# Gates behind the values' products, an output projection by single blocks, and a second norm summed inside the second FFN chunk

## The chip, the cores and the metric

The kernel runs on one core of one Trainium2 chip. The metric is the time of one execution on the device in microseconds. The median of three runs of the kernel before is 382.78 us (382.38 to 382.90).

## What is computed

A decoder layer for 256 tokens of 1,024 channels, all in float32. With one layer, one sequence and a block of 256 tokens, both attentions are plain causal softmax attentions over the 256 tokens:

```python
h = rms_norm(x, attn_norm_g)
qa, ka, va, qb, kb, vb, f_logit, g_logit = split(h @ w_in)      # 6 x 512, 8, 2 x 1024 columns
o_a = attention(rope(norm(qa)), rope(norm(ka)), va)              # 8 heads of 64, "MoBA"
o_b = attention(norm(qb), norm(kb), vb, bias=cumsum(log_sigmoid(f_logit + b_forget)))   # 8 heads, "FoX"
gates = sigmoid(g_logit + b_gate)                                # two gates for each channel
merged = gates[0] * (o_a @ w_branch_moba) + gates[1] * (o_b @ w_branch_fox)
x = x + merged @ w_out
h2 = rms_norm(x, ffn_norm_g)
u, g = split(h2 @ w_ffn_up)                                      # 2 x 2816 columns
x = x + (silu(causal_conv3(g)) * u) @ w_ffn_down
```

## The kernel before

Every large product is done in the type float32r with operands split in two: `hi` is the operand copied to float32r, `lo` is what the copy lost, and three products (hi·hi, hi·lo, lo·hi) are added in PSUM. Activations lie with channels on the partitions and the 256 tokens along the row, so that weights are the 128x128 stationary operand and a product moves 256 columns. In the first projections (q, k, v) it is the other way round, with 512 columns.

Weights come in chunks of 1 MB (128 x 2048), by one DMA each on SyncE's queue, into one of three buffers `raw`. A chunk is split in two halves, each by ScalarE (`whi`, line 122) and VectorE (`wlo`, line 123). Six buffers of each hold split halves, and `use()` asks for splits five halves ahead of the one that TensorE works on. The list `chunks` gives the order: q, k and v, eight gate chunks `wg`, four of the branch projection `wb`, four of the output projection `wo`, then the FFN, 22 `wu` and 11 `wd`. Each half chunk is 24 products of 256 columns.

TensorE's order is written out by hand (`manual_schedule`): its instructions run in the order in which the program names them. For the other engines a planner orders the instructions by the order in the program and by when its own model has their operands ready. Tiles of one tag share a number of buffers; PSUM has eight banks of 128 x 512 float32, all of the tag `bank`.

The steps around the change are these, in the names of the code.

- `scores(br, pair)`: the score products of two heads (lines 381 and 382), then the softmax on VectorE and ScalarE into a tile `s`.
- `turn(br, pair)`: six transposes of `s` (line 404), which ScalarE copies to `pT`.
- `values(br, pair)`: eight products of V and `pT` (line 415), split to `oh` and `ol` (lines 417 and 418).
- `gate(c)`: one gate chunk through `twin`, 48 products (lines 439 to 441), then a product with the first norm's factors on VectorE (446). The sigmoids of line 450 are held back behind the last exponential.
- `turn_qk`: transposes of normalized q or k (line 276), split by ScalarE (282, 286) and VectorE (288) to `qA`, `qB` and `kA`.
- The branch projection, lines 527 to 544, writes `mh` and `ml`. The output projection, lines 549 to 577, does four chunks: `c` in 0 and 1 cover the first four channel blocks of the operand for all outputs, `c` in 2 and 3 the other four. A pair of 128-channel output blocks shares one bank. When a pair is finished, VectorE adds the residual (566), ScalarE writes `hh` (569) and VectorE `hl` (570), the split operand of the FFN; ScalarE squares (572) and GpSimd adds the squares up in `sqs` (574 to 577).
- `up(f)`: one FFN chunk through `twin`, 48 products on `hh` and `hl`. The second norm's factor is not applied to the operand but to the result (line 591). After the first chunk one float32 product (588) of a matrix of ones with `sqs` sums over the channels, and `rsqrt_mean` makes `rs2` of it.
- `down(p)`: 48 products (lines 622 to 624) for two chunks of activations, added up in five banks that stay taken to the end.

The written-out order of turns, values, scores and gates stands in lines 487 to 522. The functions that the diff touches:

Of the kernel before, what the change touches and what calls it, by code (L numbers as in the profile page):

```python
# [17 lines left out]
P = 128  # L18
# [23 lines left out]
def decoder_block(ctx, tc, a, out):  # L42
# [7 lines left out]
    def T(shape, tag, bufs=1, dt=F32):  # L50
        return sb.tile(shape, dt, tag=tag, bufs=bufs, name=tag)
# [17 lines left out]
    nc.scalar.preload_act_table_set("natural_log_exp_and_others")  # L69

# [67 lines left out]
    def col(c, n=1):  # L138
        return sm[:, c:c + n]
# [268 lines left out]
    def values(br, pair):  # L408
        pT = probs.pop((br, pair))
        op = bank()  # L410
        for i, c in enumerate((slice(0, 256), slice(256, 384))):
            for j in range(2):
                o = HD * j
                vc = br * W4 + (2 * pair + j) * HD
                nc.tensor.matmul(op[o:o + HD, i * P:S], V[:, i, vc:vc + HD], pT[:, j, c], start=(i == 0), stop=(i == 1))
        b = 4 * br + pair
        nc.scalar.activation(oh[:, b], op[:, 0:S], AF.Copy)
        nc.vector.tensor_tensor(ol[:, b], op[:, 0:S], oh[:, b].bitcast(F32), op=ALU.subtract)
# [8 lines left out]
            nc.tensor.matmul(rp[:, t * P:(t + 1) * P], rs[:, t:t + 1].to_broadcast([P, P]), ident, start=True, stop=True)  # L427
        nc.vector.tensor_copy(rsB, rp[:, 0:S])

    def twin(kind, c, dst, mh, ml):  # L430

        for h in range(2):
            wh, wl = use((kind, c), h)
            for i in range(2):
                o = dst[:, i * S:(i + 1) * S]
                for k4 in range(4):
                    k = 4 * h + k4
                    w = slice(k4 * 256 + i * P, k4 * 256 + (i + 1) * P)
                    nc.tensor.matmul(o, wh[:, w], mh[:, k], start=(k == 0 and i == 0), stop=False)  # L439
                    nc.tensor.matmul(o, wh[:, w], ml[:, k], start=False, stop=False)  # L440
                    nc.tensor.matmul(o, wl[:, w], mh[:, k], start=False, stop=(k == KT - 1 and i == 1))  # L441
# [104 lines left out]

    hh = T([P, KT, S], "oh", 1, F32R)
    hl = T([P, KT, S], "ol", 1, F32R)
    acc = [bank() for _ in range(4)]
    x1 = xT  # L550
    sqs = T([P, S], "sqs")
    for c in range(4):
        for h in range(2):
            wh, wl = use(("wo", c), h)
            j = 2 * (c % 2) + h
            for i in range(2):
                o = acc[j][:, i * S:(i + 1) * S]
                for k4 in range(4):
                    k = 4 * (c // 2) + k4
                    w = slice(k4 * 256 + i * P, k4 * 256 + (i + 1) * P)  # L560
                    nc.tensor.matmul(o, wh[:, w], mh[:, k], start=(k == 0 and i == 0), stop=False)
                    nc.tensor.matmul(o, wh[:, w], ml[:, k], start=False, stop=False)
                    nc.tensor.matmul(o, wl[:, w], mh[:, k], start=False, stop=(k == KT - 1 and i == 1))
            if c >= 2:
                xx = x1[:, 2 * j:2 * j + 2]
                nc.vector.tensor_tensor(xx, acc[j].rearrange("p (b t) -> p b t", b=2), xx, op=ALU.add)
                for b in (2 * j, 2 * j + 1):
                    g = col(C_G2 + b)
                    nc.scalar.activation(hh[:, b], x1[:, b], AF.Copy, scale=g)
                    nc.vector.scalar_tensor_tensor(hl[:, b], x1[:, b], g, hh[:, b].bitcast(F32), op0=ALU.mult, op1=ALU.subtract)  # L570
                sq = T([P, 2, S], "sq", 2)
                nc.scalar.activation(sq, xx, AF.Square)
                if j == 0:
                    nc.gpsimd.tensor_tensor(sqs, sq[:, 0], sq[:, 1], op=ALU.add)
                else:
                    nc.gpsimd.tensor_tensor(sqs, sqs, sq[:, 0], op=ALU.add)
                    nc.gpsimd.tensor_tensor(sqs, sqs, sq[:, 1], op=ALU.add)
    sp = bank()
    rs2 = T([P, S], "rs2")


    acts = {}

    def up(f):
        up_ = bank()
        twin("wu", f, up_, hh, hl)
        if f == 0:
            nc.tensor.matmul(sp[:, 0:S], ones, sqs, start=True, stop=True)
            rsqrt_mean(rs2, sp[:, 0:S], D, [S], "pT")
        ev = T([P, 2, S], "sq", 2)  # L590
        nc.vector.tensor_tensor(ev, up_.rearrange("p (b t) -> p b t", b=2), rs2[:, None, :].to_broadcast([P, 2, S]), op=ALU.mult)  # L591
# [7 lines left out]
        nc.vector.tensor_tensor(av, u, sl, op=ALU.mult)  # L599
# [3 lines left out]
        nc.scalar.activation(ah, av, AF.Copy)  # L603
        nc.vector.tensor_tensor(al, av, ah.bitcast(F32), op=ALU.subtract)
# [99 lines left out]
```

## Time and profile before

| what | value |
|---|---|
| median of three runs | 382.78 us |
| the profiled execution | 382.86 us |
| its span, first to last instruction | 381.0 us |
| mean granted TensorE clock | 1.000 |
| TensorE products (PE) busy | 375.2 us, 98% of the span, 2,893 instructions |
| TensorE weight loads (PEld) busy | 353.7 us, 93% |
| VectorE (DVE) busy | 287.3 us, 75% |
| ScalarE (ACT) busy | 228.2 us, 60% |
| GpSimd (POOL) busy | 17.3 us, 5% |
| HBM | 67.13 MB read, 179 GB/s over the span with what is written |

A row of the timeline gives the start in microseconds from the span's start, the duration, the engine, the line of the kernel, the operation with output and input tiles, its shape, how many instructions are merged in the row, and in brackets the idle time before it with what ended that. Products on TensorE overlap each other: a row of 0.28 us does not mean that the next product starts 0.28 us later, so their rate is read from their starts. A row of the waits gives who waited for whom, the total in microseconds, how often, and the longest. Rows of the chain that ended last give a start, a duration, and what ran.

### The profile page before, as it was taken

The numbers are of one execution on the slowest core, as the hardware profiler recorded it, in microseconds if no ns is written. First come the engines' busy times: TensorE is split into PE (matmuls) and PEld (weight loads), VectorE is DVE, ScalarE is ACT, GpSimd is POOL, SyncE is SP. The second block draws the span as 40 slices with busy tenths as digits, with TensorE's granted clock in tenths as the row PEclk, the third lists the DMA queues.
The fourth block names the chain that finished last, engine by engine and source line by source line (L and its number), as shares of the span: only waits on it lengthen the run. The fifth ranks groups of instructions, "written<-read, shape, count | busy, mean of one in ns | idle before, by whom it ended". The sixth has DMA issues, their size and how long they took to land.

```text
span 381.0 us, 7095 instructions
## 1 busy us (share of the span) xinstructions
PE 375.2 (98%) x2893; PEld 353.7 (93%) x2893; DVE 287.3 (75%) x504; ACT 228.2 (60%) x385; POOL 17.3 (5%) x19
## 2 busy tenths in 40 slices
PE   8999999999999999999999999999999999999996
PEld 4887878889999999999989999999999999999996
DVE  4989999898988646895969967667676767667553
ACT  5947796759866974553877545455464544545520
POOL 2430000000000000000340000000000000000000
PEclk9999999999999999999999999999999999999999
DMA  8977633555164344456545445545545555645002
GB/s 284 389 267 272 227 110 111 222 221 200 65 232 169 110 157 178 120 212 222 199 143 212 165 175 214 189 151 213 192 150 212 201 154 199 221 138 196 2 0 110
DMA packets 11424, 68.63 MB, mean 180 GB/s; under 512 B 1528, under 2 KB 1920, under 8 KB 3968
## 3 DMA queue, kind: packets, MB, share of 16 engines
q1 hardware_dynamic: 11088, 67.13, 49.5%
q10 hardware_dynamic: 304, 1.06, 0.7%
q8 instruction: 22, 0.36, 0.4%
q14 instruction: 10, 0.08, 0.1%
HBM read 67.13 MB, written 1.06 MB: 179 GB/s over the span
## 4 chain that ended last, share of the span: by engine, by line
PE 73%; ACT 10%; DVE 9%; DMA 3%; issue 2%; POOLq 0%; SPq 0%; POOL 0%; ACTq 0%; DVEq 0%
PE bank L440 13%; PE bank L439 13%; PE bank L441 13%; PE bank L623 5%; PE bank L624 5%; PE bank L622 5%; DVE wlo L123 5%; PE bank L231 4%; ACT whi L122 3%; PE bank L535 2%; PE bank L537 2%; PE bank L536 2%; DMA raw<-in_lead 2%; ACT qA L286 1%; ACT qA L282 1%
## 5 line engine op out<-in xcount | busy, mean ns | idle before, releaser
L123 DVE TENSOR_TENSOR wlo<-raw,whi 128x1024 fp32r<-128x1024 f32 (+1 forms) x126 | 152.8, 1217 | 51.1 <-ACT whi L122 49.8
L122 ACT ACTIVATE whi<-raw 128x1024 fp32r<-128x1024 f32 (+1 forms) x126 | 128.5, 1027 | 86.3 <-PE bank L440 51.2
L440 PE MATMUL bank<-ol,whi 128*128 128x256 f32 x352 | 99.0, 281 | 0.1
L439 PE MATMUL bank<-oh,whi 128*128 128x256 f32 x352 | 99.0, 281 | 0.0
L441 PE MATMUL bank<-oh,wlo 128*128 128x256 f32 x352 | 98.9, 281 | 0.0
L439 PEld LDWEIGHTS bank<-oh,whi 128*128 128x128 f32 x352 | 67.5, 192 | 0.0
L440 PEld LDWEIGHTS bank<-ol,whi 128*128 128x128 f32 x352 | 66.1, 188 | 0.3 <-DVE ol L570 0.3
L441 PEld LDWEIGHTS bank<-oh,wlo 128*128 128x128 f32 x352 | 66.1, 188 | 0.0
L439 PE MATMUL bank<-xh,whi 128*128 128x256 f32 x128 | 36.1, 282 | 0.0
L440 PE MATMUL bank<-xl,whi 128*128 128x256 f32 x128 | 35.7, 279 | 0.0
L441 PE MATMUL bank<-xh,wlo 128*128 128x256 f32 x128 | 35.7, 279 | 0.0
L231 PE MATMUL bank<-whi,xh 128*128 128x512 f32 x80 | 25.4, 399 | 0.0
L231 PE MATMUL bank<-wlo,xh 128*128 128x512 f32 x80 | 25.1, 395 | 0.0
L231 PE MATMUL bank<-whi,xl 128*128 128x512 f32 x80 | 24.9, 393 | 0.0
L441 PEld LDWEIGHTS bank<-xh,wlo 128*128 128x128 f32 x128 | 24.3, 190 | 0.0
L439 PEld LDWEIGHTS bank<-xh,whi 128*128 128x128 f32 x128 | 24.1, 188 | 0.2 <-issue 0.2
L440 PEld LDWEIGHTS bank<-xl,whi 128*128 128x128 f32 x128 | 24.0, 188 | 0.0
L591 DVE TENSOR_TENSOR sq<-bank,rs 128x512 f32<-128x512 f32 x22 | 15.1, 691 | 8.9 <-PE bank L441 8.9
L390 ACT ACTIVATE s<-s,nm 128x128 f32<-128x128 f32 (+1 forms) x32 | 14.2, 448 | 8.5 <-DVE nm L387 8.5
L231 PEld LDWEIGHTS bank<-wlo,xh 128*128 128x128 f32 x80 | 15.0, 188 | 3.6 <-DVE wlo L123 0.3
L231 PEld LDWEIGHTS bank<-whi,xl 128*128 128x128 f32 x80 | 15.0, 188 | 3.4
L622 PE MATMUL bank<-qA,whi 128*128 128x256 f32 x64 | 18.0, 281 | 0.0
(180 smaller groups left out, 782.2 us busy)
## 6 DMA issues: line engine op xcount, KB each, us to landing
raw<-in_wu SPq DMA_DIRECT2D x22, 1024.0 KB, 4.8
raw<-in_wd SPq DMA_DIRECT2D x11, 1024.0 KB, 4.8
raw<-in_qkv SPq DMA_DIRECT2D x8, 1024.0 KB, 4.8
raw<-in_wg SPq DMA_DIRECT2D x8, 1024.0 KB, 4.8
raw<-in_wb SPq DMA_DIRECT2D x4, 1024.0 KB, 4.8
raw<-in_wo SPq DMA_DIRECT2D x4, 1024.0 KB, 4.8
raw<-in_qkv SPq DMA_DIRECT2D x4, 512.0 KB, 8.2
raw<-in_lead SPq DMA_DIRECT2D x2, 640.0 KB, 6.8
```

Of the source, the lines that this page charges most:

```text
L122: nc.scalar.activation(hi[:, s], raw[:, s], AF.Copy)
L123: nc.vector.tensor_tensor(lo[:, s], raw[:, s], hi[:, s].bitcast(F32), op=ALU.subtract)
L231: nc.tensor.matmul(pt[t], lhs[:, k, t * P:(t + 1) * P], rhs, start=(k == 0 and i == 0), stop=(k == KT - 1 and i == 2))
L390: last_exp[:] = [nc.scalar.activation(s[:, j, c], s[:, j, c], AF.Exp, scale=-1.0, bias=nm[:, j, i:i + 1], accum_out=l[:, j, i:i + 1])]
L439: nc.tensor.matmul(o, wh[:, w], mh[:, k], start=(k == 0 and i == 0), stop=False)
L440: nc.tensor.matmul(o, wh[:, w], ml[:, k], start=False, stop=False)
L441: nc.tensor.matmul(o, wl[:, w], mh[:, k], start=False, stop=(k == KT - 1 and i == 1))
L535: nc.tensor.matmul(o, wh[:, w], oh[:, 4 * br + k], start=(k == 0), stop=False)
L591: nc.vector.tensor_tensor(ev, up_.rearrange("p (b t) -> p b t", b=2), rs2[:, None, :].to_broadcast([P, 2, S]), op=ALU.mult)
L622: nc.tensor.matmul(o, wh[:, w], ah, start=(p == 0 and h == 0 and c == 0), stop=False)
L623: nc.tensor.matmul(o, wh[:, w], al, start=False, stop=False)
L624: nc.tensor.matmul(o, wl[:, w], ah, start=False, stop=(last and h == 1 and d == ds[-1]))
```

## The change

Five things change. In the written-out order of the attention stage, turns and scores come ahead of the values in most places, so that gates 0, 1, 2, 5, 6 and 7 directly follow a values group. In the output projection each of the eight output blocks has a bank of its own (its first 256 columns), and the residual, `hh` and `hl` are done when a block is finished, not a pair. The second half of the first FFN chunk takes its operand blocks in two steps, blocks 4 and 5 for both outputs and then 6 and 7. The norm's sum is no longer one float32 product after the first chunk: `sqs` is split like an operand into `sqr`, and two float32r products of a matrix of ones (`onesr`, made from the constants by one ScalarE copy) stand between the halves of the second FFN chunk. They write the unused half of the fifth of the down projection's banks. The first two chunks are activated after both are multiplied; from the third on each chunk is activated as before. Two tiles are new: `onesr` is placed between the split weights and the split operands, `sqr` behind `kA`.

```diff
+    T([P, P], "onesr", 1, F32R)
     gap("gap1", GAPS[1])
...
+    T([P, 2, S], "sqr", 1, F32R)
...
+    onesr = T([P, P], "onesr", 1, F32R)
+    nc.scalar.activation(onesr, ones, AF.Copy)
...
-    def twin(kind, c, dst, mh, ml):
+    def twin(kind, c, dst, mh, ml, late=False, between=None):
         for h in range(2):
             wh, wl = use((kind, c), h)
-            for i in range(2):
+            if between and h:
+                between()
+            steps = [(i, k4) for ks in (((0, 1), (2, 3)) if late and h else ((0, 1, 2, 3),)) for i in range(2) for k4 in ks]
+            for i, k4 in steps:
                 o = dst[:, i * S:(i + 1) * S]
-                for k4 in range(4):
-                    k = 4 * h + k4
...
     finish_v(pv, 1)
+    turn(0, 2)
     values(0, 1)
-    turn(0, 2)
     forget_bias()
     gate(0)
     turn(0, 3)
     turn_qk(kn, 1, 1)
     values(0, 2)
     gate(1)
+    scores(1, 0)
     values(0, 3)
-    scores(1, 0)
     gate(2)
     scores(1, 1)
     gate(3)
     turn(1, 0)
     scores(1, 2)
     gate(4)
-    values(1, 0)
     turn(1, 1)
     scores(1, 3)
+    values(1, 0)
     gate(5)
+    turn(1, 2)
     values(1, 1)
-    turn(1, 2)
     gate(6)
+    turn(1, 3)
     values(1, 2)
-    turn(1, 3)
     gate(7)
...
-    acc = [bank() for _ in range(4)]
+    acc = [bank()[:, 0:S] for _ in range(KT)]
...
             for i in range(2):
-                o = acc[j][:, i * S:(i + 1) * S]
+                b = 2 * j + i
+                o = acc[b]
...
-            if c >= 2:
-                xx = x1[:, 2 * j:2 * j + 2]
-                nc.vector.tensor_tensor(xx, acc[j].rearrange("p (b t) -> p b t", b=2), xx, op=ALU.add)
-                for b in (2 * j, 2 * j + 1):
+                if c >= 2:
                     g = col(C_G2 + b)
+                    nc.vector.tensor_tensor(x1[:, b], o, x1[:, b], op=ALU.add)
                     nc.scalar.activation(hh[:, b], x1[:, b], AF.Copy, scale=g)
                     nc.vector.scalar_tensor_tensor(hl[:, b], x1[:, b], g, hh[:, b].bitcast(F32), op0=ALU.mult, op1=ALU.subtract)
+            if c >= 2:
                 sq = T([P, 2, S], "sq", 2)
-                nc.scalar.activation(sq, xx, AF.Square)
+                nc.scalar.activation(sq, x1[:, 2 * j:2 * j + 2], AF.Square)
...
+    def norm2():
+        sqr = T([P, 2, S], "sqr", 1, F32R)
+        nc.scalar.activation(sqr[:, 0], sqs, AF.Copy)
+        nc.vector.tensor_tensor(sqr[:, 1], sqs, sqr[:, 0].bitcast(F32), op=ALU.subtract)
+        sp = acc[4][:, S:2 * S]
+        for i in range(2):
+            nc.tensor.matmul(sp, onesr, sqr[:, i], start=(i == 0), stop=(i == 1))
+        rsqrt_mean(rs2, sp, D, [S], "pT")
 
     def up(f):
         up_ = bank()
-        twin("wu", f, up_, hh, hl)
-        if f == 0:
-            nc.tensor.matmul(sp[:, 0:S], ones, sqs, start=True, stop=True)
-            rsqrt_mean(rs2, sp[:, 0:S], D, [S], "pT")
+        twin("wu", f, up_, hh, hl, f == 0, norm2 if f == 1 else None)
+        return up_
+
+    def activate(f, up_):
...
     for j in range(NF // 2):
-        up(2 * j)
-        up(2 * j + 1)
+        pair = []
+        for f in (2 * j, 2 * j + 1):
+            pair.append(up(f))
+            if j > 0:
+                activate(f, pair.pop())
+        if j == 0:
+            for f in range(2):
+                activate(f, pair[f])
         if j > 0:
             down(j - 1)
```

More of the change, by code (lines that the diff above doesn't have):

```diff
@@ L428, in rs_row @@
         nc.vector.tensor_copy(rsB, rp[:, 0:S])
-    def twin(kind, c, dst, mh, ml):
+    def twin(kind, c, dst, mh, ml, late=False, between=None):
         for h in range(2):
             wh, wl = use((kind, c), h)
-            for i in range(2):
+            if between and h:
+                between()
+            steps = [(i, k4) for ks in (((0, 1), (2, 3)) if late and h else ((0, 1, 2, 3),)) for i in range(2) for k4 in ks]
+            for i, k4 in steps:
                 o = dst[:, i * S:(i + 1) * S]
-                for k4 in range(4):
-                    k = 4 * h + k4
[L438 to L441, printed above, removed]
+                k = 4 * h + k4
+                w = slice(k4 * 256 + i * P, k4 * 256 + (i + 1) * P)
+                nc.tensor.matmul(o, wh[:, w], mh[:, k], start=(k == 0 and i == 0), stop=False)
+                nc.tensor.matmul(o, wh[:, w], ml[:, k], start=False, stop=False)
+                nc.tensor.matmul(o, wl[:, w], mh[:, k], start=False, stop=(k == KT - 1 and i == 1))
     def gate(c):
@@ L560, in decoder_block @@
                     w = slice(k4 * 256 + i * P, k4 * 256 + (i + 1) * P)
[L561 removed]
+                    nc.tensor.matmul(o, wh[:, w], mh[:, k], start=(k == 0), stop=False)
                     nc.tensor.matmul(o, wh[:, w], ml[:, k], start=False, stop=False)
[L563 to L567 removed]
+                    nc.tensor.matmul(o, wl[:, w], mh[:, k], start=False, stop=(k == KT - 1))
+                if c >= 2:
                     g = col(C_G2 + b)
+                    nc.vector.tensor_tensor(x1[:, b], o, x1[:, b], op=ALU.add)
                     nc.scalar.activation(hh[:, b], x1[:, b], AF.Copy, scale=g)
                     nc.vector.scalar_tensor_tensor(hl[:, b], x1[:, b], g, hh[:, b].bitcast(F32), op0=ALU.mult, op1=ALU.subtract)
+            if c >= 2:
                 sq = T([P, 2, S], "sq", 2)
[L572 removed]
+                nc.scalar.activation(sq, x1[:, 2 * j:2 * j + 2], AF.Square)
                 if j == 0:
```

1 line of the change is left out of this document (removed).

## Prediction

> **What bounds the kernel now.** I read the profile in this order: the busy shares on the page, the granted clock, the waits of the tensor engine, then the timeline of TensorE alone at every place where the change moves something, and last the other engines around the second norm.
>
> ```profile
> span 381.0 us, 7095 instructions
> PE 375.2 (98%) x2893; PEld 353.7 (93%) x2893; DVE 287.3 (75%) x504; ACT 228.2 (60%) x385; POOL 17.3 (5%) x19
> ...
> core 0: 381.0 us, clock 1.000
> ...
> PEld bank L588 <- POOL sqs L577: 0.6, 1, 0.6
> ...
> PEld bank L381 <- DVE kA L288: 0.3, 1, 0.3
> ```
>
> TensorE is busy nearly throughout at the full granted clock, and its waits in the region of the change are tenths of a microsecond. If the change only took waits away, it could bring about one microsecond of 381. So the next question is whether TensorE, while busy, always goes equally fast. It does not, and this is the main point. The rows below are boundaries of runs of 48 identical products (one gate chunk: 128x128 weights, 256 columns), with what stood ahead of each: L415 are the values' products, L404 a turn's transposes, L381/L382 scores.
>
> ```profile
> 94.80 0.87 PE L415 MATMUL bank<-pT,V 128*64 128x256 f32 x8
> 95.60 0.39 PE L439 MATMUL bank<-xh,whi 128*128 128x256 f32 x1
> ...
> 101.25 0.87 PE L415 MATMUL bank<-pT,V 128*64 128x256 f32 x8
> ...
> 103.08 0.38 PE L381 MATMUL bank<-kA,qA 128*128 128x256 f32 x1
> ...
> 103.43 0.28 PE L439 MATMUL bank<-xh,whi 128*128 128x256 f32 x1
> ...
> 108.87 0.22 PE L381 MATMUL bank<-kA,qA 128*128 128x128 f32 x1
> ...
> 124.98 0.28 PE L439 MATMUL bank<-xh,whi 128*128 128x256 f32 x1
> ...
> 130.73 0.87 PE L415 MATMUL bank<-pT,V 128*64 128x256 f32 x8
> 131.53 0.87 PE L404 MATMUL bank<-cst,s 128*128 128x128 f32 x6
> 132.16 0.36 PE L439 MATMUL bank<-xh,whi 128*128 128x256 f32 x1
> ...
> 137.99 0.87 PE L415 MATMUL bank<-pT,V 128*64 128x256 f32 x8
> ...
> 139.42 0.36 PE L439 MATMUL bank<-xh,whi 128*128 128x256 f32 x1
> ...
> 145.25 0.87 PE L415 MATMUL bank<-pT,V 128*64 128x256 f32 x8
> 146.05 0.39 PE L535 MATMUL bank<-oh,whi 128*128 128x256 f32 x1
> ```
>
> Directly after values, gate 1 takes 95.60 to 101.25, 5.65 us. After turns, gates 6 and 7 take 132.16 to 137.99 and 139.42 to 145.25, 5.83 us each. After scores it goes either way: gate 2 takes 5.44 (103.43 to 108.87; TensorE had just waited at 103.08), gate 5 takes 5.75 (124.98 to 130.73). So the same product has a short and a long spacing, and the spacing is kept until something else intervenes. The next rows show how long.
>
> ```profile
> 189.69 0.28 PE L439 MATMUL bank<-oh,whi 128*128 128x256 f32 x1
> ...
> 193.09 0.28 PE L439 MATMUL bank<-oh,whi 128*128 128x256 f32 x1
> 193.49 0.38 PE L440 MATMUL bank<-ol,whi 128*128 128x256 f32 x1
> 193.71 0.28 PE L441 MATMUL bank<-oh,wlo 128*128 128x256 f32 x1
> ...
> 193.94 0.33 PE L440 MATMUL bank<-ol,whi 128*128 128x256 f32 x1
> 194.11 0.28 PE L441 MATMUL bank<-oh,wlo 128*128 128x256 f32 x1
> ...
> 195.52 0.28 PE L441 MATMUL bank<-oh,wlo 128*128 128x256 f32 x1
> 196.21 0.70 PE L588 MATMUL bank<-sqs,cst 128*128 128x256 f32 x2 [0.41 <-POOL sqs L577]
> 196.56 0.47 PE L439 MATMUL bank<-oh,whi 128*128 128x256 f32 x1
> 196.87 0.28 PE L440 MATMUL bank<-ol,whi 128*128 128x256 f32 x1
> ...
> 377.70 0.13 PE bank L624
> ```
>
> From 146.05, right behind the last values, to 193.09 lie 192 products of the branch projection, 192 of the output projection and 30 of the first FFN chunk: 47.04 us over 414, 113.6 ns each. Then come a wait for hl, the norm's float32 product L588, and from 196.56 to the end of the last down product at 377.70 the other 1,536 products of the FFN (22 chunks of 48 and 11 of 48, less the first 48): 181.14 us, 117.9 ns each. The difference is 4.3 ns, and 1,536 times that is 6.6 us. What stands ahead of the FFN is worth more than every wait in the kernel.
>
> **The change part by part.** The profiled execution took 382.86 us, span 381.0 and 1.86 around it; the median of the runs is 382.78, so nothing has to be converted.
>
> *Gates behind values.* No product is added. Gates 6 and 7 now follow values instead of a turn: 5.83 to 5.65, twice -0.18. Gate 5 follows values instead of scores: -0.10. Gate 2 follows values where it had a scores group after a wait: +0.21. Gates 3 and 4 keep what stands ahead of them. Gate 0 also gains 0.18, but ahead of a wait (next), so it counts zero. Sum -0.25.
>
> *Scores(1,0) ahead of values(0,3).* Now values(0,3) run at 101.25 and fill 0.80 us (like 94.80 to 95.60) that TensorE would otherwise wait for kA. Its producer:
>
> ```profile
> 102.27 0.76 DVE L288 SCALAR_TENSOR_TENSOR kA<-bank,sm,kA 64x512 fp32r<-64x512 f32 x1
> ...
> 191.23 0.68 DVE L566 TENSOR_TENSOR xT<-bank,xT 128x512 f32<-128x512 f32 x1
> ...
> 192.96 0.87 DVE L570 SCALAR_TENSOR_TENSOR ol<-xT,sm,oh 128x256 fp32r<-128x256 f32 x2
> ...
> 202.67 1.28 DVE L591 TENSOR_TENSOR sq<-bank,rs 128x512 f32<-128x512 f32 x2
> ...
> 194.51 1.65 POOL L577 TENSOR_TENSOR sqs<-sqs,sq 128x256 f32<-128x256 f32 x1
> ...
> 195.72 1.06 ACT L122 ACTIVATE whi<-raw 128x1024 fp32r<-128x1024 f32 x1 [1.40 <-PE bank L440]
> ...
> 219.31 0.42 ACT L603 ACTIVATE qB<-s 128x256 fp32r<-128x256 f32 x1 [1.31 <-DVE s L599]
> ...
> 219.76 0.43 DVE L604 TENSOR_TENSOR qB<-s,qB 128x256 fp32r<-128x256 f32 x1 [0.49 <-ACT qB L603]
> ```
>
> kA is written until 103.03 and the scores' last pair starts at 103.08. With scores first, they still end there, and the values come behind: +0.80. If the planner brings kA forward by as much, zero; with gate 0's gain lost as well, +1.0. I take 0.80, since the same DVE and ACT work stands ahead of kA as before. Behind this wait on TensorE stand values(0,3) and every later gate; the softmaxes have microseconds to spare (scores of one pair are turned more than a gate later).
>
> *Output projection by single blocks.* The same 192 products. Four additions of 0.68 become eight of about 0.43: DVE gets 0.7 us more in all, but block 2j can be added while block 2j+1 is still multiplied, half a chunk earlier. DVE was 1.5 us behind at the last pair (addition at 191.23, the projection over at 189.69). The late order in the first chunk's second half moves the first use of k=6 from behind 30 products to behind 36, 0.68 us later (193.8; hl is written from 192.96 on). The wait from 193.09 to 194.11 is five spacings in 1.02 us instead of 0.57; I remove it whole: -0.45, bound by +0.5 of new wait if DVE ends 0.7 later. Eight accumulators take all eight PSUM banks; the first chunk must then wait for one addition. Any block but the last two is added before 189.69; I count zero, and were it the last, up to 2.
>
> *The norm's products.* L588 goes: from 195.52 to 196.87 two spacings (0.23) lay where 1.35 us passed, so -1.12 with its wait. Two products of the stream's own form come in: +0.23. They stand after 72 products, at 189.69 + 72 x 0.1136 = 197.87. sqs is ready at 194.51 + 1.65 = 196.16; ACT's copy (like 0.42) and DVE's subtraction (like 0.43) follow, 197.0 if nothing is in their way; a weight split on each engine (1.06, about 1.2) may be, which gives 199.2. I take a wait of 0.3, between zero and 1.2. Behind the waiting products stand the chunk's second half and all later chunks; behind the copy and the subtraction, which wait for sqs and for each other, stand weight splits that are needed five half chunks later, so their lateness is covered. The reciprocal root then ends some 1.5 us later than now; its first reader stood at 202.67, and the third chunk's bank covers that: TensorE has 72 more products, 8 us, before it needs a bank back.
>
> *onesr.* One ACT copy, shorter than 0.42.
>
> ```profile
> 10.07 0.43 SPq L175 DMA_DIRECT2D cst<-in_consts  x1
> ...
> 23.52 0.20 ACT L189 ACTIVATE rsv<-rsv 128x2 f32<-128x2 f32 x1 [4.15 <-DVE rsv L188]
> ```
>
> ACT idles 4.15 us before 23.52, after the constants have come, so it costs nothing; uncovered it costs 0.4. Were it queued ahead of weight splits it would hold them until the constants land; the weights' DMAs are issued ahead of those on the same queue, so I leave that out. No DMA is moved: the loads follow the chunks, whose order stays.
>
> *The FFN's spacing.* The two products are no different from their neighbours, so nothing changes the spacing by its form; what remains is waits. A wait so long that weights and product start together (193.49, 146.05 and 95.60 show it: a first product of 0.38 to 0.39 and the next 0.22 later) led into the short spacing each time. The short one at 193.94 led into the long one. So a wait of 0.3 or more or none keeps 113.6 ns: -6.6. The other bound is 0.
>
> The Trainium skill, "TensorE: Matmul & The Clock Gate", section "Back-to-back issue gap", gives the gap between warm products by columns and clock alone, about 109 ns for 256 columns. The trace gives 113.6 and 117.9 at one granted clock, so here it disagrees; by that rule the FFN's term would be zero and the sum 382.4.
>
> Sum: 382.86 - 0.25 + 0.80 - 0.45 - 1.12 + 0.23 + 0.3 - 6.6 = **375.8 us**. With the bounds: 374.5 (no wait at the scores, none at the norm, gate 3 also short) to 377.4 (1.0 at the scores, 0.5 at hl, 1.2 at the norm).
>
> **The rivals.** *The FFN stays at the long spacing.* A short wait, below one spacing, at hl or between the two products flips it as at 193.94. For it: hl has only about 0.4 us in hand, and the subtraction comes within a microsecond of its use. Against it: the window is 0.1 us wide, and 414 products in a row kept the short spacing through three different stages. Time: 375.8 + 6.6 = 382.4 (381.1 to 384.0). The Trainium skill's page named above leads here too.
>
> *ACT's queue holds the norm.* The weight split traced ahead of the copy waits for the first half of that same chunk (the split at 195.72 waited 1.40 us for such a release). If the planner puts it first, it starts at 197.87, ends 198.93, the copy 199.35, the subtraction 199.8, or 201 behind a split on DVE: TensorE waits 1.8 to 3.0 us rather than 0.3. The wait is long, so the spacing stays short: 377.9.
>
> *The long spacing everywhere.* onesr moves the tiles xh, xl, oh, ol and those behind to other addresses by 512 bytes. If the short spacing hangs on where operands lie and not on what went before, all that is short now can turn long: gates 1, 2 and 4 and 414 products, 558 x 4.3 ns = 2.4 us, with no gain at gates or FFN: 382.86 + 0.80 - 1.04 + 2.4 = 385.0, slower. Against it: today both spacings occur with the same tiles. It is decided by gate 1: 5.65 or 5.85.
>
> **How the numbers follow.** Forecast 0.57, FFN long 0.20, ACT's queue 0.14, long everywhere 0.09. A difference of 0.2% (0.8 us) is about what a measurement of this kernel can tell. Faster: 0.57 + 0.14 and a quarter of the second case, 0.76; same: half of the second, 0.11 with rounding; slower 0.13. The range goes from 374.5 to 382.6, so far into the second case that 2 in 10 stay out; the likeliest case's own is 374.5 to 377.4.
>
> **What would show it.** Right: every FFN chunk about 5.45 us, gates 5 to 7 near 5.6, no float32 pair of 0.70 us at the norm, TensorE waiting about 1.2 us for kA. Wrong: 118 ns between products of the third chunk or later, waits of over 1.5 us at the two products, or gate 1 above 5.8 us.

## The result and the profile after

| | runs | median, us | all, us |
| --- | --- | --- | --- |
| before | 4 | 382.84 | 382.38, 382.78, 382.9, 383.06 |
| changed | 4 | 379.46 | 379.08, 379.43, 379.49, 385.3 |

The ratio is 0.991 (95% interval 0.989 to 0.9929). The forecast of 375.8 asked for -7.0; these runs gave -3.4, and one of the four is 5.8 us above the other three. That run turned out to be the clue: later repetitions of both kernels fall into two groups of times each, about 6.5 us apart. Over all runs of this study:

| kernel | lower group | upper group |
| --- | --- | --- |
| before, 40 executions | 12 at 375.55 to 376.63 | 28 at 382.13 to 383.5 |
| changed, 10 executions | 8 at 379.05 to 379.49 | 2 at 385.3 and 385.56 |

The four runs of before shown above all lie in its upper group, and three of the four of the changed kernel in its lower group. The granted clock is 0.998 to 1.000 in profiles of either group. So -3.4 compares unlike with unlike; by the medians of the groups the change is slower, by 3.4 us in the lower ones (375.8 and 379.2) and 2.6 in the upper ones. The comparison of the lower groups on one chip, taken with a later run, gives 1.0085 (1.007 to 1.0099). The means of all executions (380.7 and 380.5) say little, since each hangs on how many executions happened to fall into which group: their standard errors are 0.5 and 0.8 us.

The page of the changed kernel's profiled execution (379.49 us, 1.79 of it outside the span), with the costliest FFN group:

```profile
span 377.7 us, 7097 instructions
PE 370.6 (98%) x2893; PEld 349.4 (93%) x2893; DVE 288.8 (76%) x509; ACT 228.9 (61%) x387; POOL 15.4 (4%) x19
...
L445 PE MATMUL bank<-oh,whi 128*128 128x256 f32 x352 | 97.5, 277 | 0.0
```

The busy share hides everything: 98% as before. What moved is the spacing of equal products, and it moved both ways. The windows view of TensorE alone counts products in a stretch (columns: stretch, its length, PE busy and products, clock, DMA share, GB/s; a product across an edge counts, so two or three more appear than fit). Before:

```profile
155.00:185.00 30.00, 30.00 (x267) 1.00 0.59 206
225.00:285.00 60.00, 60.00 (x512) 1.00 0.52 183
```

Changed:

```profile
155.00:185.00 30.00, 30.00 (x257) 1.00 0.50 178
225.00:285.00 60.00, 60.00 (x532) 1.00 0.55 193
```

267 products in 30 us is the short spacing (113.3 ns), 257 the long one (117.8 ns); 532 in 60 us is short, 512 long. Before, the projections are short and the FFN is long. In the changed kernel it is the other way round. The starts of the stages, from the timeline of TensorE, show what each place gave and took:

| from - to | before, us | changed, us | difference |
| --- | --- | --- | --- |
| span's start - branch projection | 146.05 | 147.11 | +1.06 |
| branch projection - first FFN chunk | 43.64 | 45.33 | +1.69 |
| first - second FFN chunk | 6.87 | 5.65 | -1.22 |
| second FFN chunk - first down product | 17.15 | 17.20 | +0.05 |
| first down product - fifth FFN chunk | 5.66 | 6.70 | +1.04 |
| fifth FFN chunk - last product | 158.17 | 152.20 | -5.97 |

The three places that cost are these rows of the changed kernel's timeline, TensorE alone:

```profile
95.94 0.39 PE L445 MATMUL bank<-xh,whi 128*128 128x256 f32 x1 [0.36 <-DVE qB L292]
...
103.17 0.38 PE L385 MATMUL bank<-kA,qA 128*128 128x256 f32 x1 [0.63 <-DVE kA L292]
...
146.31 0.87 PE L419 MATMUL bank<-pT,V 128*64 128x256 f32 x8
147.11 0.38 PE L541 MATMUL bank<-oh,whi 128*128 128x256 f32 x1
147.33 0.28 PE L542 MATMUL bank<-ol,whi 128*128 128x256 f32 x1
...
215.29 0.33 PE L637 MATMUL bank<-qA,whi 128*128 128x256 f32 x1
216.53 0.38 PE L638 MATMUL bank<-qA,whi 128*128 128x256 f32 x1 [0.92 <-DVE qA L619]
```

At 95.94 gate 1 waits for VectorE's last subtraction into `qB`, which ends at 95.89, and then runs long. Gate 1 does not read `qB`; by the code, what it can be waiting for is the bank that the subtraction reads. In the kernel before, the same subtraction ended at 96.02, and gate 1 had started at 95.60 without a wait. At 103.17 the scores wait for kA. From 147.11, right behind values, 578 products run long until 215.29; before, 414 products at the same place ran short. At 216.53 the second product of the first down chunk starts 1.24 us after the first, 1.13 more than the spacing, because it waits for the low half of the activation. From there the other 1,390 products run short. The waits of the weight loads name the operands of the first down chunk and of the scores first in the region of the change:

```profile
PEld bank L638 <- DVE qA L619: 1.1, 1, 1.1
PEld bank L385 <- DVE kA L292: 0.8, 1, 0.8
```

Why the first down chunk has to wait now is a chain on VectorE and ScalarE, here VectorE's part with two rows of ScalarE:

```profile
198.38 0.41 DVE L593 TENSOR_TENSOR sqr<-sqs,sqr 128x256 fp32r<-128x256 f32 x1
...
201.00 1.06 ACT L124 ACTIVATE whi<-raw 128x1024 fp32r<-128x1024 f32 x1 [1.76 <-PE bank L446]
202.07 1.28 ACT L193 ACT_TABLE_LOAD   x1
...
201.35 0.42 DVE L192 TENSOR_SCALAR pT<-bank 128x256 f32<-128x256 f32 x1 [0.86 <-PE bank L596]
...
206.47 0.42 DVE L197 SCALAR_TENSOR_TENSOR rs<-pT 128x256 f32<-128x256 f32 x1
...
207.95 1.28 DVE L606 TENSOR_TENSOR sq<-bank,rs 128x512 f32<-128x512 f32 x2
...
216.06 0.75 DVE L619 TENSOR_TENSOR qA<-s,qA 128x256 fp32r<-128x256 f32 x2
```

The norm's products (L596, at 200.92) are not kept waiting: `sqr` is complete at 198.79. But the reciprocal root takes from 201.35 to 206.89, 5.5 us instead of 4.7 (196.95 to 201.61), since a weight split on ScalarE stands ahead of the root's first table load. So the first activation starts at 207.95 instead of 202.67, 5.3 us later by the clock; 2.75 of that is the whole stream being late at the FFN (192.44 instead of 189.69), and 2.5 is the norm's own. The activation needs 8.9 us to its last result at 216.81. Before, there were 11.0 us from 202.67 to the first down product at 213.71; now there are 7.3 (207.95 to 215.29).

### The profile page after: what moved, and what is told of

Its sections match the earlier page's. It is cut to its first block, busy times and chain, and to the rows that moved or that the text cites. A ratio compares the mean times of both kernels' runs of the same rounds, so it can differ in the third digit from the quotient of the medians.

```text
span 377.7 us, 7097 instructions
## 1 busy us (share of the span) xinstructions
PE 370.6 (98%) x2893; PEld 349.4 (93%) x2893; DVE 288.8 (76%) x509; ACT 228.9 (61%) x387; POOL 15.4 (4%) x19
## 3 DMA queue, kind: packets, MB, share of 16 engines
q10 hardware_dynamic: 304, 1.06, 0.7%
HBM read 67.13 MB, written 1.06 MB: 181 GB/s over the span
## 4 chain that ended last, share of the span: by engine, by line
PE 73%; DVE 10%; ACT 9%; issue 3%; DMA 3%; SPq 0%; ACTq 0%; DVEq 0%
PE bank L445 13%; PE bank L447 12%; PE bank L446 12%; PE bank L638 5%; PE bank L639 5%; DVE wlo L125 5%; PE bank L637 5%; PE bank L235 4%; ACT whi L124 3%; PE bank L541 2%; PE bank L542 2%; PE bank L569 2%; PE bank L568 2%; PE bank L570 2%; PE bank L543 2%
## 5 line engine op out<-in xcount | busy, mean ns | idle before, releaser
L445 PE MATMUL bank<-oh,whi 128*128 128x256 f32 x352 | 97.5, 277 | 0.0
L446 PE MATMUL bank<-ol,whi 128*128 128x256 f32 x352 | 97.5, 277 | 0.0
L447 PE MATMUL bank<-oh,wlo 128*128 128x256 f32 x352 | 97.5, 277 | 0.0
L445 PEld LDWEIGHTS bank<-oh,whi 128*128 128x128 f32 x352 | 66.2, 188 | 0.0
```

## The experiments

Two theories stood on record before the first of these kernels ran. By the restart theory the spacing is drawn anew wherever TensorE's stream is interrupted, by where in a grid of a few nanoseconds it starts again, and then lasts. By the predecessor theory, the prediction's, what stands ahead decides: values or a long wait give the short spacing. A third possibility is that the parts of the change have a fixed price each. The first four kernels take the parts one by one. Short below means 113.3 ns a product, long 117.8.

**Gates alone** (before, with only the new order of the attention stage).

```diff
+    turn(0, 2)
     values(0, 1)
-    turn(0, 2)
...
+    scores(1, 0)
     values(0, 3)
-    scores(1, 0)
...
+    turn(1, 3)
     values(1, 2)
-    turn(1, 3)
```

> The kernel before with the new order of turns, values, scores and gates alone. Restart theory (the spacing of the products, 113.3 or 117.8 ns, is drawn anew wherever TensorE's stream is interrupted, by where in a grid of a few nanoseconds it starts again, and then lasts): the branch projection starts 1.0 us later than before, as in the changed kernel; branch and output projection at either spacing; behind the float32 product of the norm the FFN most likely long as before: 383.8, or 385.7 with the projections long; if a restart falls well, 377. Predecessor theory (the record's: values ahead of a stream give the short spacing): gates 0, 1, 2, 5, 6, 7 and the projections short, FFN long: 383.4.

Measured: 378.24 in the profiled execution, then 384.95, 385.29 and 385.33. Its windows:

```profile
155.00:185.00 30.00, 30.00 (x257) 1.00 0.52 179
200.00:210.00 10.00, 10.00 (x91) 1.00 0.44 151
225.00:285.00 60.00, 60.00 (x532) 1.00 0.56 193
```

The new order alone turns the projections long (415 products from 147.01). It also shows that the FFN can run short behind the float32 product L588, which the gates' order does not touch. A median of two such unlike values says nothing, which is why the executions are listed from here on.

**Single blocks alone** (before, with one bank, addition and split for each output block).

```diff
-    acc = [bank() for _ in range(4)]
+    acc = [bank()[:, 0:S] for _ in range(KT)]
...
-            if c >= 2:
-                xx = x1[:, 2 * j:2 * j + 2]
-                nc.vector.tensor_tensor(xx, acc[j].rearrange("p (b t) -> p b t", b=2), xx, op=ALU.add)
-                for b in (2 * j, 2 * j + 1):
+                if c >= 2:
+                    nc.vector.tensor_tensor(x1[:, b], o, x1[:, b], op=ALU.add)
```

> The kernel before with the output projection by single blocks alone. The order of attention stays, so the branch projection starts at 146.0 and is short as before. Both theories: up to 0.45 us less waiting for hl, the float32 product of the norm stays: 382.3 to 382.9. Restart theory alone allows 376 where the restart at the norm's product falls well; predecessor theory: FFN long behind a float32 product.

Measured: 382.69, 382.18, 382.56, 382.31. TensorE at the first FFN chunk:

```profile
193.05 0.28 PE L439 MATMUL bank<-oh,whi 128*128 128x256 f32 x1
193.60 0.39 PE L440 MATMUL bank<-ol,whi 128*128 128x256 f32 x1 [0.27 <-DVE ol L569]
...
193.94 0.28 PE L439 MATMUL bank<-oh,whi 128*128 128x256 f32 x1
194.48 0.38 PE L440 MATMUL bank<-ol,whi 128*128 128x256 f32 x1 [0.26 <-DVE ol L569]
```

Single blocks do not take the wait for `hl` away: two gaps of 0.55 us remain, where before had one of 0.40 and one of 0.17. All four times are those of a long FFN, as the profiled one is.

**Norm alone** (before, with the float32r products, the late order and `onesr`; old attention order, paired output projection).

```diff
+        nc.scalar.activation(sqr[:, 0], sqs, AF.Copy)
+        nc.vector.tensor_tensor(sqr[:, 1], sqs, sqr[:, 0].bitcast(F32), op=ALU.subtract)
...
+            nc.tensor.matmul(sp, onesr, sqr[:, i], start=(i == 0), stop=(i == 1))
...
+        twin("wu", f, up_, hh, hl, f == 0, norm2 if f == 1 else None)
```

> The kernel before with the norm's two products in the second FFN chunk, the late order in the first, and the first two activations after both chunks; attention order and output projection as before. Both theories: the stream that is short from 146.0 on meets no float32 product; without a wait it stays short into the third FFN chunk. Restart theory: every wait on the way (hl, the norm's products, the first down product) draws anew, so 375.5 to 376.5 where the last draw is short, 381 to 382.5 where it is long. Predecessor theory: 375.5 to 376.5.

Measured, ten executions: six at 375.94 to 377.01, four at 382.01 to 382.79; the profiled one is among the four (382.67). Against before's lower group the lower group is 1.0019 (1.0005 to 1.0032). In its trace 577 products run short from 146.35 to the first down product, without a break; then:

```profile
211.64 0.28 PE L447 MATMUL bank<-oh,wlo 128*128 128x256 f32 x1
212.25 0.38 PE L637 MATMUL bank<-qA,whi 128*128 128x256 f32 x1 [0.34 <-ACT qA L618]
213.56 0.39 PE L638 MATMUL bank<-qA,whi 128*128 128x256 f32 x1 [0.92 <-DVE qA L619]
213.78 0.28 PE L639 MATMUL bank<-qA,wlo 128*128 128x256 f32 x1
```

Two waits, of 0.5 and 1.2 us beyond the spacing, and then 1,390 products long. In the changed kernel a wait of the same kind at the same instruction led into the short spacing. So "a long wait leads into the short spacing" falls, and the same kernel gives both outcomes.

**Down later** (the changed kernel, with the first down chunk behind the sixth FFN chunk instead of the fourth, loads and products alike).

```diff
-        if j > 0:
-            down(j - 1)
+        if j == 2:
+            down(0)
+        if j > 1:
+            down(j - 1)
```

> The changed kernel with the first down product and its weights two FFN chunks later (beside the second), so that TensorE does not wait there for the activations (1.25 us at 215.3 in the changed kernel). Restart theory: the stream that became long at the branch projection (147.1) is not interrupted any more, so the whole FFN is long: 379.5 - 1.1 + 6.1 = 384.5, slower than before by 0.4%. Rival: the FFN's short spacing comes from the norm's products or from the order of the FFN, and the wait is a plain cost: 378.3.

Measured: 384.75, 384.15, 384.25, 384.09. The wait is gone, one uninterrupted run of 1,969 products reaches from 147.67 to the end, and all of it is long:

```profile
155.00:185.00 30.00, 30.00 (x257) 1.00 0.52 178
300.00:360.00 60.00, 60.00 (x511) 1.00 0.47 168
```

Taking a wait of 1.1 us away made the kernel 5 us slower than the changed kernel's lower group, as the restart theory had it (384.5), where the rival had 378.3. This is the strongest sign that spacing is a matter of the last interruption: with none behind the branch projection, its long spacing is kept to the end, and there is only one group of times.

The restart theory is carried further from here. Where TensorE is interrupted by its own instructions alone, the draw is the same each time; where it waits for another engine, it differs between executions. The rival: the execution as a whole is in a short or a long condition.

**Norm and down later** (the norm part with the old attention order and paired output projection, and the down chunk later as above). Theory: the old order draws short at the branch projection, nothing interrupts behind it, so one group only and all short.

> The kernel before with the norm's part of the change (as e3_norm_only) and the first down product two chunks later. Restart theory: the branch projection starts short at 146, as in every kernel with the old attention order, and nothing interrupts TensorE from there to the end, so no draw is left: every execution short, e3's short executions (about 376.4) less its wait of 1.7 us at the down product: 374.7 in all of them, within 0.3. Rival (an execution as a whole is in one of two states): again two groups of times, near 374.7 and 381.5.

Measured: 373.83, 374.36, 374.16, 374.89, 374.31, 375.13. One group in six executions, and the fastest kernel of the study: its median of 374.34 is 8.5 us under before's median of 382.84, and 1.5 under before's lower group (median 375.8). The six spread over 1.3 us, more than the 0.3 on either side that was expected. The timeline at the branch projection and the windows:

```profile
144.45 0.87 PE L421 MATMUL bank<-pT,V 128*64 128x256 f32 x8
145.25 0.39 PE L543 MATMUL bank<-oh,whi 128*128 128x256 f32 x1
145.48 0.28 PE L544 MATMUL bank<-ol,whi 128*128 128x256 f32 x1
```

```profile
155.00:185.00 30.00, 30.00 (x267) 1.00 0.58 208
300.00:360.00 60.00, 60.00 (x532) 1.00 0.40 142
```

The run of 1,969 products from 145.48 to the end is short throughout. It differs from the one before (384.2) in the order of attention and the blocks of the output projection, none of which lies in the FFN, where most of the 10 us arise. The load on the DMA engines does not go with the spacing: their share is 0.58 and 0.40 in the two stretches of this short run, and 0.52 and 0.47 in the long run of the kernel before it.

**Last turn moved** (down later, with the last turn behind gate 7, so that gate 7 and what follows it restart otherwise).

```diff
-    turn(1, 3)
     values(1, 2)
     gate(7)
+    turn(1, 3)
```

> e4_down_later with the last turn moved from before the seventh gate's values to behind gate 7, so that the branch projection follows turn and values from a long gate 7. Restart theory with a spacing that TensorE's own sequence hands on (long stream, turn, values gives short at gates 6 in all kernels with the new order; short stream, values gives long at the branch projection): gate 7 long, branch projection and all behind it short to the end: 384.2 - 1,969 x 4.4 ns = 375.6. Rival (the new order as such, or the blocks, make the projection and the FFN long): 384.2.

Measured: 377.43, 377.21, 385.81, 385.59. In the profiled execution the branch projection is short (423 products from 148.63), as the theory wanted, but the values ahead of it now wait 0.81 us for ScalarE, and with the faster projections TensorE waits for `hl` again (a gap of 0.43 us at 196.48). Both are waits for another engine, and there are two groups again. The single-group forecast missed, by a wait that the forecast had not counted. No execution of the upper group was profiled; the 8.4 us between the groups are nearer to 1,968 long products (8.7, or 8.4 without the wait for `hl`) than to the 1,545 behind the wait for `hl` (6.9), which points at the wait ahead of the branch projection.

**Norm again** (the norm part once more, unchanged, for its second draw).

> e3_norm_only unchanged, for a second profile. Restart theory: the same program up to 213 us product by product, and behind the wait at the first down product either spacing: 376.4 with 113.3 ns to the end, or 382.7 with 117.8. Rival (an execution as a whole is in one state): where the time is 376.4, the products before 213 us differ from e3's profile too.

Measured: 383.26. The trace repeats the first one: short from 146.93, waits of 0.5 and 1.2 us at the first down product, long behind them. It did not catch an execution of the lower group, so it adds a second case and no contrast.

**Old order, single blocks, down later** (norm and down later, with the single blocks put in).

> The changed kernel with the old attention order and the first down product two chunks later: e5_norm_down_later with the output projection by single blocks. Restart theory: short from 146 to the end in every execution, unless the blocks bring a wait for hl: 374.7, or a little below. A wait for hl would draw anew: two groups, 375 and 381.5.

Measured: 374.89, 374.85, 381.18, 374.61, 374.64, 374.98. The wait for `hl` is back:

```profile
193.94 0.28 PE L447 MATMUL bank<-oh,whi 128*128 128x256 f32 x1
194.36 0.39 PE L448 MATMUL bank<-ol,whi 128*128 128x256 f32 x1
194.58 0.28 PE L449 MATMUL bank<-oh,wlo 128*128 128x256 f32 x1
```

A gap of 0.42 us instead of 0.11, and with it one execution of six in an upper group. So single blocks cost about 0.3 us here and bring a wait back; that they bring the draw back with it fits, but one of six against none of six is too few to show it. The wait is for the last block of `hl`: DVE's split of it takes 0.96 us here and ends at 194.31, just before the product, and takes 0.48 and ends at 193.03 with paired blocks (norm and down later). From each kernel's first FFN product, at 189.52 and 188.89, that is 4.8 us and 4.1. In the changed kernel, where the output projection and the first FFN chunk run long, the split ends 4.3 us behind the first FFN product, and the wait is not seen. This kernel and "down later" (384.2) differ in the attention order alone: the order decides whether the stream behind it starts short.

**Gates again, change again** (both kernels repeated on one chip).

> e1_gates_only unchanged, for a second profile of it. Its first profile (378.2) had the long spacing from 147 us to the norm and the short one behind; its three other executions took 385.1. Restart theory: the same products at the same spacing up to the wait for hl at 196 us, and behind the waits there either spacing: 385.1 with 117.8 ns to the end, or 378.2 again. Rival (an execution as a whole is in one state): where the time is 385.1, the stages before 196 us differ too.

> The changed kernel unchanged, for more executions beside the kernel before. Restart theory: one draw that matters, at the first down product: two groups, 379.3 (most) and 385.4; the kernel before two groups, 375.9 and 382.6. Predecessor theory of the record: one group each.

Measured: gates 384.32; the change 379.05, 385.56, 379.23, 379.14, 379.27, 379.24. The windows of the gates' second trace:

```profile
155.00:185.00 30.00, 30.00 (x257) 1.00 0.55 186
200.00:210.00 10.00, 10.00 (x87) 1.00 0.55 184
225.00:285.00 60.00, 60.00 (x512) 1.00 0.52 192
```

Beside the first trace of the same kernel: all eight gates and the projections agree in their spacing, and the 13 products between the `hl` wait and L588 are short in both. Behind L588 one goes short and the other long, and keeps it for 1,535 products. A condition of the whole execution is thereby refuted: the two executions are alike up to the last wait for another engine, and part there. The two were taken on different chips, but on the first one alone the four executions had already fallen into both groups. The starts on either side, first the earlier trace, then this one:

```profile
198.41 0.70 PE L588 MATMUL bank<-sqs,cst 128*128 128x256 f32 x2 [0.47 <-POOL sqs L577]
198.76 0.47 PE L439 MATMUL bank<-oh,whi 128*128 128x256 f32 x1
199.06 0.28 PE L440 MATMUL bank<-ol,whi 128*128 128x256 f32 x1
```

```profile
197.71 0.70 PE L588 MATMUL bank<-sqs,cst 128*128 128x256 f32 x2 [0.48 <-POOL sqs L577]
198.06 0.47 PE L439 MATMUL bank<-oh,whi 128*128 128x256 f32 x1
198.36 0.28 PE L440 MATMUL bank<-ol,whi 128*128 128x256 f32 x1
```

At the view's 10 ns these rows show the same pattern: 0.35 and 0.30 us from start to start in both, after waits of 0.47 and 0.48. What decides is finer.

**Without the late order** (norm and down later, first FFN chunk in the old order of blocks).

```diff
-        twin("wu", f, up_, hh, hl, f == 0, norm2 if f == 1 else None)
+        twin("wu", f, up_, hh, hl, False, norm2 if f == 1 else None)
```

> e5_norm_down_later without the late order in the first FFN chunk, so that TensorE waits for hl again at 193 us (0.45 us before). Restart theory: that wait draws the spacing for the 1,545 products behind it: two groups, 374.8 and 381.4. Rival (only the float32 product and the wait at the down product matter): one group at 374.8.

Measured: 382.12 (the profiled one), 375.4, 381.06, 375.25, 375.4, 381.34. A wait for `hl` (a gap of 0.40 us at 193.26) returns, the FFN behind it is long in the profiled execution, and three of six executions are in each group. The lower group is 1 us above that of norm and down later, of which the wait explains about 0.45 (193.26 to 194.29, five spacings); the rest was not traced, and the two were run on different chips. So the late order is worth up to 1 us by itself and 4 us in the mean of six (378.4 and 374.4); most of the 4 is that no execution fell into an upper group.

## Why the prediction was right or wrong

*The reading that stands.* TensorE bounds the kernel, two spacings of the same product exist, and 4.4 ns times the FFN's products is the largest term in the kernel: the row from the fifth FFN chunk to the end gives -5.97 for 1,344 products, 4.4 ns each. That before's FFN was long was true of the execution that the sum started from. But the -5.97 did not come by the path that was forecast. The stream was to arrive short from the projections and stay short; it arrived long, and turned short only at a wait that the sum did not have. That wait has either outcome, so collecting this term was luck. By the prediction's own signs it was wrong: the third and fourth FFN chunks run at 117.8 ns a product. That 379.5 lies between 374.5 and 382.6 is luck as well: the upper bound came from a rival, the long FFN, which is not what this execution shows.

*The step that failed first* is the rule "directly after values the spacing is short", with its companion, that a wait long enough to start weights and product together "led into the short spacing each time". It was drawn from three shown restarts. In the changed kernel six gates and the branch projection follow values: gates 0, 2, 6 and 7 run short, gates 1 and 5 and the branch projection restart just so, with a first product of 0.38 to 0.39, and run long. The norm alone waits 1.2 us and runs long behind it. The sum had taken the 414 products of the branch and output projections as short, unchanged; they cost +1.69 instead of zero, and the same long run goes on to the first down product, so that of the forecast -6.6 some 0.64 were not collected there (the 144 products of the second to fourth FFN chunks x 4.4 ns).

*The term that was not in the sum* is the first down chunk's wait, 1.13 us in the trace. The prediction saw that the reciprocal root comes later ("ends some 1.5 us later than now"; it was 5.3 us, 201.61 to 206.89, or 2.5 us against TensorE's own stream), and said that the third chunk's bank covers it. It looked only at when a bank is needed back and not at the next reader down the chain, the activation that the first down product reads.

*Gates and scores.* Forecast +0.55 together, measured +1.06. The wait for kA was sized too high: it rose from 0.3 to 0.8 us in the waits, +0.5, where the sum had +0.80 and the sign asked for 1.2. Gates 2, 6 and 7 are short as forecast, and gate 5 is long. Not foreseen were gate 1's wait (0.36 idle) and its long spacing, which put its last product 0.53 later (101.05 and 101.58), and gate 4, which the sum took as unchanged: it went from 113.5 to 117.8 ns a product, +0.2.

*L588, the late order, the norm's products.* Forecast -1.12, -0.45, +0.23 and +0.3. Of the -1.12, 0.93 lie in the row from the first to the second FFN chunk (195.52 to 196.56 of before, less one spacing); with -0.45 that is -1.38, and -1.22 was measured, with some 0.15 of long spacing in it (48 long products for 13). The rest, -0.19, and +0.23 for the two products come out in the next row as +0.05. These terms hold. The wait of 0.3 at the norm's products did not come: they stood at 200.92, the copy and subtraction were done at 198.79. The rival in which ScalarE's queue holds the norm did not occur either (its wait, by its own terms 199.8 or 201 less 197.87, would have been 1.9 to 3.1 us, not 1.8 to 3.0). "The wait for hl goes" holds in the changed kernel, but by a cover that was not named: the blocks bring it back as soon as the projections run short (the kernel with old order and blocks), and it is the late order that removes it with paired blocks (the kernel without it).

*"The FFN stays long"* was given 0.20 and occurred in 2 of 10 executions, at 385.3 and 385.56 and not 382.4. Neither was profiled. Their distance of 6.2 us from the lower group is that of the 1,390 products behind the first down product's wait (1,390 x 4.44 ns = 6.2), so the draw lay most likely there and not at `hl`; that the share agrees with the chance is an accident. *"The long spacing everywhere"* was priced at 385.0 and named gate 1 as the sign. Gate 1 was long (117.7 ns a product from 96.17 on), and yet the FFN was short. Addresses do not explain it: with the same tiles and addresses gate 1 is long in the first trace of the changed kernel and short in the second.

*The page of the Trainium skill.* "TensorE: Matmul & The Clock Gate", section "Back-to-back issue gap", gives one gap for a warm product of a given width, by a formula that it calls that of an isolated product. Every trace here has two, 113.3 and 117.8 ns, at a granted clock of 0.998 to 1.000; the measurement decides. By that rule the forecast would have been 382.4, which none of the ten executions gave.

*The measure itself.* One execution of a kernel with a wait for another engine in front of the FFN is one draw from two groups. The prediction took before's 382.8 for a fixed quantity, and 0.8 us for what a measurement of this kernel can tell. Like for like (lower groups, 375.8 and 379.2), the change costs 3.4 us. By the rows above, with before's FFN thought short behind L588 (no profile caught before in its lower group): +1.06 and +1.69, about -1.1 at L588, +0.64 for three chunks that would have been short (144 x 4.45 ns), and +1.25 at the first down chunk, which would have been short in both (its wait and restart), together 3.5.

What stays open: why the old order draws short at the branch projection and the new one long goes with the phase described below, but the phase was not set on purpose; no kernel shifted a restart by a chosen nanosecond or two.

## What to carry to other kernels

Judge a busy engine by start to start of equal instructions, stage by stage, and count over several executions how the times group before a difference of 1 or 2% is believed: the same program can be 6.5 us apart by one draw. A wait ahead of a long uniform stream is worth removing for the draw more than for its own length, but only if the stream then starts from a place that sets the short spacing: the same edit (down later) gave 384.2 behind one order and 374.3 behind another. When a producer is moved later, follow the chain to every reader, not to the next one.

## What the runs showed of the hardware

Products of 256 columns in float32r, each with its own weight load, run at 113.33 or 117.78 ns at the same granted clock, and keep it until something interrupts the stream, for up to 1,969 products. Both fit a grid of 6.67 ns: 17 steps are a short product, and three long ones take 353.3 ns, 53 steps. The short runs of one trace, though interruptions lie between them, stand at the same point of this grid within 0.45 ns in every trace (within a run of 400 products or more the concentration of the phases is 0.95 to 0.97, where 1 is perfect).

Over the thirteen traces there are 62 restarts of a gate, a projection or an FFN stream whose second product follows the first after 221 to 226 ns. Sorted by where in half a grid step (3.33 ns, against the phase that all short runs of the trace have in common) the first product starts, from the traces' nanosecond starts, which are finer than the rows above:

| phase of the first product, ns | short | long |
| --- | --- | --- |
| 0.0 to 0.44 | 0 | 10 |
| 0.6 to 0.8 | 2 | 1 |
| 1.3 to 2.7 | 41 | 1 |
| 2.9 to 3.31 | 4 | 3 |

A start well between two points of the half grid goes short, with one exception in 42 (the norm alone, at 213.56). The first and the last row lie equally near a point, one behind it and one ahead of it: together 13 long and 4 short, so near a point both occur. The starts are whole nanoseconds, so the table cannot draw a finer line. Left out are seven restarts at the scores near 103 us, where the gate behind them breaks the stream once more, and one stream of 14 products; all eight go short, two of the scores from 0.09 and 0.34 ns.

It is a correlation over traces, not something that a kernel set. It fits the rest. Where TensorE follows its own instructions the phase repeats: the branch projection starts at 1.3 to 2.1 ns and is short in all seven traces of the old attention order, and starts within 0.4 ns of a point and is long in all five of the new one (without the kernel with the last turn moved). Behind a wait for another engine it need not repeat: the second product of the first down chunk starts at 1.3 and 0.6 ns in the changed kernel's two traces and at 1.3 and 0.0 in those of the norm alone.
